# Key stacks completed by transfers inside SBUF, and sixteen attention rows scaled on another engine

## The chip, the cores and the metric

The kernel runs on one core of one Trainium2 chip. The metric is the device time of one execution in microseconds (us). Below, TensorE does matmuls (PE, its weight loads PEld), VectorE is DVE, ScalarE is ACT, GpSimd is POOL, and SyncE (SP) issues nearly all transfers (DMAs).

## What is computed

One transformer layer on 512 tokens of width 1024: a modulated layer norm, one projection to queries, keys, values and gates, two kinds of attention of 8 heads each, an output projection, a second norm and a gated feed-forward part with a short convolution. What matters here is the attention. Heads "a" use one softmax with a mask that merges three dilation patterns. Heads "b" have three branches (compressed, selected, window), each with a softmax of its own and a gate. In short:

```python
qa, ka, va, qb, kc, vc, ksl, vsl, kw, vw, gl = jnp.split(u @ w_in[l], split_at, axis=-1)
o_a = dilated_attention(partial_rope(heads(qa, N_HEADS_A), pos),
                        partial_rope(heads(ka, N_HEADS_A), pos), heads(va, N_HEADS_A))
...
s = jnp.einsum('bghqd,bgkd->bghqk', qc, kwc).astype(jnp.float32) * scale
p, _, den = masked_exp(s, wmask, -1)
o_win = jnp.einsum('bghqk,bgkd->bghqd', p, vwc) / den
o = gc[..., 0:1] * o_cmp + gc[..., 1:2] * o_slc + gc[..., 2:3] * o_win
```

## The kernel before, in words

**Products of halves.** To keep float32 accuracy a factor is split into a high part (a copy to fp32r) and a low part (the rest). The projections, which the trace calls "quad", multiply high by high, high by low and low by high (mm3, L259 to L261).

**Query and key stacks.** A head has 64 columns, so its transposed query fills 64 of 128 partitions. The kernel uses the other 64: q_stack writes the high part of a query in one half of the partitions and its low part in the other (L468 to L471). A key stack, made by k_half, holds the same key twice, once in each half of the partitions: khh has its high part twice, kll its low part twice. So one matmul with khh and one with kll, each contracting over all 128 partitions, give a row's scores (L700, L701). k_half takes the transposed key from PSUM: ScalarE writes the high part into both halves (L477, L478), VectorE subtracts to get the low part in one half (L479) and copies it into the other (L480). It is called twelve times: four times ahead of the first row (k_stack, keys of the selected and window branches for both groups), and twice for each of the head pairs a0 to a3 (in a_post, one step of the background work each).

**Rows.** A row is the work on one or two query tiles of 128 tokens of one head and branch: tiles (0, 1) with 128 + 256 = 384 score columns, tile 2 with 384, tile 3 with 512. The order of the heads is ROWS: b0, b1, a0, a1, b2, the compressed rows c, b3, a2, a3. Each of the heads b0 and b1 has 12 rows, so rows 0 to 23 are theirs, and all of them have a gate. A row goes through these steps: scores (TensorE), weights (VectorE: mask and row minimum, L708), power (ScalarE: exponential and its sum, L714), scale (VectorE: reciprocal of the sum, L719; GpSimd: times reciprocal times gate, in place, L722), turn (TensorE: transposes, L727), parts (ScalarE: high part, L746), rest (VectorE: low part, L750), use (TensorE: weighted sum of values, L775). Step k of the main loop has the scores of row k + 1, the mask and exponential of row k, the scaling of row k - 1, the transposes of row k - 3 and the weighted sum of row k - 5, and between these steps puts pieces of the projections (fill) and of the background work (misc).

**Projections and loads.** fill_stream loads a piece of w_quad into one of four raw buffers (wraw), splits it on ScalarE and VectorE (L1108, L1111) and multiplies. The same four buffers serve the modulation weights (ada_col, consumed by L1019 on VectorE; ada_row by L1010) and the compression weights (k_w, v_w). All of these loads are issued by SyncE, in order, and each waits until its buffer is free.

**Order.** The tile framework orders the instructions of each engine when the kernel is built, and sets the waits between engines. An engine then works its own list in that order.

Of the kernel before, what the change touches and what calls it, by code (L numbers as in the profile page):

```python
# [14 lines left out]
AF = mybir.ActivationFunctionType  # L15
# [91 lines left out]
def body(ctx, tc, nc, a, out, dbg=None):  # L107
# [59 lines left out]
    V, A, P, T = nc.vector, nc.scalar, nc.gpsimd, nc.tensor  # L167
# [23 lines left out]
    def q4(name, dt=F32, shape=(128, 1024)):  # L191
        return slot('q4', NQ, list(shape), dt, name)
# [16 lines left out]
    def pk(name):  # L209
        return slot('p', NP, [128, 512], F32, name)  # L210
# [22 lines left out]
    def bank(tag, name=None, shape=(128, 512)):  # L233
        return ps.tile(list(shape), F32, name=name or tag, tag=tag, bufs=BANKS[tag])

    def f(x):
        return x.bitcast(F32)

    def load(dst, src, queue=nc.sync):
        queue.dma_start(dst, src)  # L240
# [230 lines left out]
        V.tensor_sub(o[0:64], pt[64:128], f(o[64:128]))  # L471
        return e, o

    def k_half(pt, e, mk=t2):
        b, c0 = 64 * e, 64 - 64 * e
        hh, ll = mk('khh'), mk('kll')
        A.activation(hh[b:b + 64], pt[b:b + 64], AF.Copy)  # L477
        A.activation(hh[c0:c0 + 64], pt[b:b + 64], AF.Copy)  # L478
        V.tensor_sub(ll[b:b + 64], pt[b:b + 64], f(hh[b:b + 64]))  # L479
        V.tensor_copy(ll[c0:c0 + 64], f(ll[b:b + 64]))  # L480
        return hh, ll

    def k_stack(pt, mk=t2):
        return [k_half(pt, e, mk) for e in range(2)]


    gates = cst.tile([128, NT, 24], F32, name='gates')
# [194 lines left out]
    def attend(need_q, need_v, pv_of, qk_of, vsel, mask0, gate, first, last, end, f4):  # L682
# [3 lines left out]
        def row(tiles):  # L686
            cols, n = {}, 0
            for i in tiles:
                cols[i] = slice(n, n + 128 * (i + 1))
                n += 128 * (i + 1)  # L690
            pr, one = tiles[0] // 2, len(tiles) == 1
            e = {'n': n}

            def scores():
                need(*need_q)
                q, (hh, ll) = qk_of()
                e['s'] = bank('s', 'sp')
                for i in tiles:
                    qi = q[:, 128 * i:128 * i + 128]
                    T.matmul(e['s'][:, cols[i]], qi, hh[:, 0:128 * (i + 1)], start=True, stop=False)  # L700
                    T.matmul(e['s'][:, cols[i]], qi, ll[:, 0:128 * (i + 1)], start=False, stop=True)  # L701

            def weights():
                p = e['p'] = pk('p')
                m_ = e['m'] = cst.tile([128, 3, 2], F32, name='sa_', tag='sa_', bufs=5)
                for x, i in enumerate(tiles):
                    m0 = mask0 + 512 - 128 * (i + 1)
                    V.tensor_tensor_reduce(p[:, cols[i]], e['s'][:, cols[i]], masks[:, m0:mask0 + 512], 1.0, 3e38,  # L708
                                           op0=ALU.add, op1=ALU.min, accum_out=m_[:, 0, x:x + 1])

            def power():
                p, m_ = e['p'], e['m']
                for x, i in enumerate(tiles):
                    A.activation(p[:, cols[i]], p[:, cols[i]], AF.Exp, bias=m_[:, 0, x:x + 1], scale=-1.0,  # L714
                                 accum_out=m_[:, 1, x:x + 1])

            def scale():
                p, m_ = e['p'], e['m']
                V.reciprocal(m_[:, 2, 0:len(tiles)], m_[:, 1, 0:len(tiles)])  # L719
                for x, i in enumerate(tiles):  # L720
                    g = 1.0 if gate is None else gates[:, i, gate:gate + 1]
                    P.tensor_scalar(p[:, cols[i]], p[:, cols[i]], m_[:, 2, x:x + 1], g, op0=ALU.mult, op1=ALU.mult)  # L722

            def turn():
                e['t'] = bank('tr', 'pT')
                for j in range(n // 128):
                    T.transpose(e['t'][:, 128 * j:128 * j + 128], e['p'][:, 128 * j:128 * j + 128], ident)  # L727

            def side(c):
                if pr == 0:  # L730
                    return pair['h'][:, 512 * c:512 * c + 384]
                x = 128 * (tiles[0] % 2)
                return pair['hl'[c]][:, 0:n // 128, x:x + 128]

            def turned():
                t = e['t'][:, 0:n]
                return t if pr == 0 else t.rearrange("p (j q) -> p j q", q=128)

            def parts():
                if pr == 0:  # L740
                    pair['h'] = q4('pT', F32 if f4 else F32R)
                elif tiles[0] == 2:
                    pair['h'] = q4('pTh', F32 if f4 else F32R, (128, 4, 256))
                    if not f4:
                        pair['l'] = q4('pTl', F32R, (128, 4, 256))
                A.activation(side(0), turned(), AF.Copy)  # L746

            def rest():
                if not f4:
                    V.tensor_sub(side(1), turned(), f(side(0)))  # L750
                e['pair'] = dict(pair)
                if pr == 0:
                    lows.append(e['pair'])

            def use():
                if tiles[0] == LU:
                    return
                need(*need_v)
                if LU == 0 and tiles[0] == 2:
                    product_of(0, lows[0])  # L760
                else:
                    product_of(pr, e['pair'])

            def product_of(pr, tl):
                pv = pv_of()
                for j in range(2 * pr + 2):
                    o0 = 128 if j == 2 * pr + 1 else 0
                    o_ = pv[:, 256 * pr + o0:256 * pr + 256]
                    for c in range(1 if f4 else 2):
                        if pr == 0:  # L770
                            x = 512 * c + 256 * j
                            m_ = tl['h'][:, x:x + 256 - o0]
                        else:
                            m_ = tl['hl'[c]][:, j, o0:256]
                        T.matmul(o_, vsel(j), m_, start=(first and pr == 0 and j == 0 and c == 0),  # L775
                                 stop=(last and j == 3 and (f4 or c == 1)))
                if pr == 1:
                    end()

            e.update(scores=scores, weights=weights, power=power, scale=scale, turn=turn, parts=parts, rest=rest,  # L780
                     use=use)
            return e
# [257 lines left out]
    def late_steps(gap, AUX):  # L1040
        for c in AUX:
            if c == 'k':
                yield from hidden(kc_r, 'k_w1', P, comp_keys)
            if c == 'v':
                yield from hidden(vc_t, 'v_w1', P, comp_values)
            if c == 'g':
                yield from ada_row(0, g1l, gap)
            if c == 'c':
                yield from ada_late_cols(gap)
            if c == '2':  # L1050
                yield from ada_late_cols(gap, (2,))
            if c == '3':
                yield from ada_late_cols(gap, (3,))
# [10 lines left out]
    def start_misc(gen, early=False):  # L1064
        misc.insert(0 if early else len(misc), [0, gen])
# [116 lines left out]
    def need(*names):  # L1182
        while any(n not in ready for n in names):
            count(names)
            if fill_one() is fill:
                run_misc(True)
            elif tick[0] % 2:
                run_misc()
            else:
                tick[0] += 1  # L1190
# [53 lines left out]
    rows, done_b = [], []  # L1244
    for r in ROWS:
# [3 lines left out]
        else:  # L1249
            i = int(r[1])  # L1250
# [28 lines left out]
    for st_ in AUX:  # L1279
        start_misc(late_steps(GAP, st_))  # L1280
    nrow = len(rows)
    rows[0]['scores']()
    wo_started = [False]
    wo_fill = wo_first()
# [261 lines left out]
```

## Time and profile before

| | us |
|---|---|
| median of 3 runs | 726.68 |
| lowest, highest | 724.72, 728.5 |
| the profiled execution, own time | 726.39 |
| its span, first to last instruction | 724.6 |
| TensorE busy (matmuls) | 691.1 |
| VectorE busy | 464.8 |
| ScalarE busy | 345.7 |
| GpSimd busy | 248.7 |
| granted clock of TensorE, mean over the span | 0.99 |

The times of engines are sums over one profiled execution; they overlap. An engine's matmul ends are modelled, so a busy TensorE may still be slower than its peak. The granted clock is 1.00 at 2.4 GHz and 0.50 at 1.2 GHz. In the list of waits, a line names the waiting engine, its tile and line, then what ended the wait; then us in total, times, longest us. In a timeline, a line gives the start in us from the start of the span, the duration, engine, line, operation, tiles written and read, shapes, and in brackets the idle time of the engine just ahead of it with what ended it.

### The profile page before, as it was taken

How to read it: one execution, taken by the hardware profiler on the slowest of the kernel's cores; microseconds unless marked ns; L12 is line 12 of the kernel's file. 1: busy time of each engine (PE TensorE's matmuls, PEld its weight loads, DVE VectorE, ACT ScalarE, POOL GpSimd, SP SyncE). 2: the span in 40 equal slices, each digit the busy share in tenths (PEclk: the TensorE clock that was granted, in tenths of full speed). 3: DMA queues.
4: the chain of work that ended last, by engine and by line, in shares of the span. 5: the costliest groups of instructions: out<-in, count | busy, mean ns of one | idle time of the engine just before them, and what ended most of it. 6: DMA issues, size and time to landing. Idle time of an engine off the chain costs nothing.

```text
span 724.6 us, 10875 instructions
## 1 busy us (share of the span) xinstructions
PE 691.1 (95%) x3964; PEld 596.8 (82%) x3964; DVE 464.8 (64%) x961; ACT 345.7 (48%) x697; POOL 248.7 (34%) x273
## 2 busy tenths in 40 slices
PE   7999899999889998999999999999999999999995
PEld 6999788987879887778898888888888788888884
DVE  7879966766986889988843344464443364544236
ACT  5647665752767689916553333333333341222101
POOL 2002436441277475511310110111111355666216
PEclk9999999999999999999999999999999999999998
DMA  9955342046451011260112224434423233343002
GB/s 340 386 207 206 131 135 86 30 174 238 140 204 60 29 60 58 86 235 1 59 60 87 88 88 145 140 135 161 145 88 116 88 107 126 116 146 121 25 15 101
DMA packets 29149, 89.93 MB, mean 124 GB/s; under 512 B 3748, under 2 KB 4516, under 8 KB 29096
## 3 DMA queue, kind: packets, MB, share of 16 engines
q1 hardware_dynamic: 28660, 89.05, 35.6%
q8 instruction: 31, 0.51, 0.3%
q10 hardware_dynamic: 436, 0.18, 0.1%
q14 instruction: 22, 0.18, 0.1%
HBM read 87.13 MB, written 2.10 MB: 123 GB/s over the span
## 4 chain that ended last, share of the span: by engine, by line
PE 51%; DVE 3%; POOL 1%; issue 1%; ACT 0%; POOLq 0%; DVEq 0%
PE d L261 6%; PE d L260 6%; PE d L259 5%; PE pvv L259 5%; PE pvv L261 5%; PE pvv L260 5%; PE pg L259 5%; PE pg L261 5%; PE pg L260 5%; DVE x L1355 1%; PE wo L261 1%; PE wo L260 1%; PE wo L259 1%; DVE x L1346 0%; DVE bn L299 0%
## 5 line engine op out<-in xcount | busy, mean ns | idle before, releaser
L256 DVE TENSOR_TENSOR wlo<-wraw,whi 128x1024 fp32r<-128x1024 f32 x60 | 86.2, 1437 | 124.8 <-ACT whi L255 123.6
L255 ACT ACTIVATE whi<-wraw 128x1024 fp32r<-128x1024 f32 x60 | 63.6, 1060 | 142.9 <-PE pg L260 70.4
L259 PE MATMUL quad<-whi,u 128*128 128x256 f32 x256 | 75.0, 294 | 1.0 <-DVE qo L471 1.0
L260 PE MATMUL quad<-wlo,u 128*128 128x256 f32 x256 | 72.8, 284 | 0.0
L261 PE MATMUL quad<-whi,u 128*128 128x256 f32 x256 | 72.6, 284 | 0.0
L1498 POOL TENSOR_TENSOR wraw<-wraw,arow 128x1024 f32<-128x1024 f32 x22 | 57.8, 2633 | 35.3 <-DMA wraw<-w_down 28.6
L259 PE MATMUL pg<-u,whi 128*128 128x512 f32 (+1 forms) x176 | 67.7, 385 | 0.0
L260 PE MATMUL pg<-u,whi 128*128 128x512 f32 (+1 forms) x176 | 66.8, 380 | 0.0
L261 PE MATMUL pg<-u,wlo 128*128 128x512 f32 (+1 forms) x176 | 66.8, 379 | 0.0
L261 PE MATMUL pvv<-u,wlo 128*128 128x512 f32 (+1 forms) x176 | 66.8, 379 | 0.0
L259 PE MATMUL pvv<-u,whi 128*128 128x512 f32 (+1 forms) x176 | 66.8, 379 | 0.0
L260 PE MATMUL pvv<-u,whi 128*128 128x512 f32 (+1 forms) x176 | 66.8, 379 | 0.0
L256 POOL TENSOR_TENSOR hl<-cv,hh 128x512 fp32r<-128x512 f32 x14 | 23.9, 1705 | 110.8 <-ACT hh L255 110.8
L259 PEld LDWEIGHTS quad<-whi,u 128*128 128x128 f32 x256 | 48.7, 191 | 5.7 <-issue 3.9
L708 DVE CUSTOM_DVE_ANT_0 p<-sp,masks 128x128 f32<-128x128 f32 (+1 forms) x96 | 45.0, 482 | 8.8 <-PE sp L701 7.9
L260 PEld LDWEIGHTS quad<-wlo,u 128*128 128x128 f32 x256 | 48.9, 191 | 1.0 <-issue 0.4
L261 PEld LDWEIGHTS quad<-whi,u 128*128 128x128 f32 x256 | 48.9, 191 | 0.1
L727 PE MATMUL pT<-ident,p 128*128 128x128 f32 x240 | 39.8, 280 | 4.6 <-POOL p L722 4.2
L260 PEld LDWEIGHTS pg<-u,whi 128*128 128x128 f32 x176 | 33.1, 188 | 6.6 <-issue 0.5
L256 POOL TENSOR_TENSOR hg<-cv,hg 128x512 fp32r<-128x512 f32 x8 | 12.9, 1609 | 74.9 <-ACT hg L255 74.9
L259 PEld LDWEIGHTS pg<-u,whi 128*128 128x128 f32 x176 | 33.1, 188 | 6.6 <-issue 0.5
L261 PEld LDWEIGHTS pvv<-u,wlo 128*128 128x128 f32 x176 | 33.1, 188 | 6.3
(636 smaller groups left out, 1884.7 us busy)
## 6 DMA issues: line engine op xcount, KB each, us to landing
wraw<-w_up SPq DMA_DIRECT2D x44, 512.0 KB, 3.2
wraw<-w_down SPq DMA_DIRECT2D x22, 512.0 KB, 3.4
ada<-ada_col SPq DMA_DIRECT2D x32, 256.0 KB, 6.0
wraw<-w_quad SPq DMA_DIRECT2D x16, 512.0 KB, 4.9
wraw<-ada_col SPq DMA_DIRECT2D x16, 512.0 KB, 3.3
wraw<-ada_row SPq DMA_DIRECT2D x16, 512.0 KB, 3.6
x<-x SPq DMA_DIRECT2D x8, 512.0 KB, 4.8
wraw<-w_o SPq DMA_DIRECT2D x8, 512.0 KB, 3.2
```

The lines of the kernel that those rows point to most:

```text
L255: A.activation(hi, raw, AF.Copy)
L256: lo_engine.tensor_sub(lo, raw, f(hi))
L259: T.matmul(o_, sh, mh, start=start, stop=False)
L260: T.matmul(o_, sh, ml, start=False, stop=False)
L261: T.matmul(o_, sl, mh, start=False, stop=stop)
L708: V.tensor_tensor_reduce(p[:, cols[i]], e['s'][:, cols[i]], masks[:, m0:mask0 + 512], 1.0, 3e38, op0=ALU.add, op1=ALU.min, accum_out=m_[:, ...
L727: T.transpose(e['t'][:, 128 * j:128 * j + 128], e['p'][:, 128 * j:128 * j + 128], ident)
L1355: V.scalar_tensor_tensor(src[:, hs], src[:, hs], ag[:, 3:4], b_[h][:, cs], op0=ALU.mult, op1=ALU.add)
L1498: P.tensor_mul(w, w, g2)
```

## The change

k_half gets an argument `spare`, true for all calls. With it the second copies of khh and kll aren't written by ScalarE and VectorE: a transfer issued by SyncE copies the finished half of 64 partitions to the other half, 64 x 512 values of 4 bytes, 128 KB. Over twelve calls 12 ScalarE and 12 VectorE copies go, and 24 transfers come. In scale, rows 4 to 19 take another way: VectorE multiplies the reciprocal by the gate (one small instruction for each row, as all these rows have a gate), and ScalarE multiplies each tile by that value, in place. GpSimd's instruction for these rows goes.

```diff
--- before.py
+++ after.py
@@ -471,8 +471,15 @@
         V.tensor_sub(o[0:64], pt[64:128], f(o[64:128]))
         return e, o
 
-    def k_half(pt, e, mk=t2):
+    def k_half(pt, e, mk=t2, spare=True):
         b, c0 = 64 * e, 64 - 64 * e
+        if spare:
+            hh, ll = mk('khh'), mk('kll')
+            A.activation(hh[b:b + 64], pt[b:b + 64], AF.Copy)
+            load(f(hh[c0:c0 + 64]), f(hh[b:b + 64]))
+            V.tensor_sub(ll[b:b + 64], pt[b:b + 64], f(hh[b:b + 64]))
+            load(f(ll[c0:c0 + 64]), f(ll[b:b + 64]))
+            return hh, ll
         hh, ll = mk('khh'), mk('kll')
         A.activation(hh[b:b + 64], pt[b:b + 64], AF.Copy)
         A.activation(hh[c0:c0 + 64], pt[b:b + 64], AF.Copy)
@@ -717,6 +724,13 @@
             def scale():
                 p, m_ = e['p'], e['m']
                 V.reciprocal(m_[:, 2, 0:len(tiles)], m_[:, 1, 0:len(tiles)])
+                if e['act']:
+                    if gate is not None:
+                        g = gates[:, tiles[0]:tiles[-1] + 1, gate:gate + 1].rearrange("p t o -> p (t o)")
+                        V.tensor_mul(m_[:, 2, 0:len(tiles)], m_[:, 2, 0:len(tiles)], g)
+                    for x, i in enumerate(tiles):
+                        A.activation(p[:, cols[i]], p[:, cols[i]], AF.Copy, scale=m_[:, 2, x:x + 1])
+                    return
                 for x, i in enumerate(tiles):
                     g = 1.0 if gate is None else gates[:, i, gate:gate + 1]
                     P.tensor_scalar(p[:, cols[i]], p[:, cols[i]], m_[:, 2, x:x + 1], g, op0=ALU.mult, op1=ALU.mult)
@@ -1279,6 +1293,8 @@
     for st_ in AUX:
         start_misc(late_steps(GAP, st_))
     nrow = len(rows)
+    for k, r in enumerate(rows):
+        r['act'] = 4 <= k < 20
     rows[0]['scores']()
     wo_started = [False]
     wo_fill = wo_first()
```

## Rows read from the trace of the kernel before

**Rows 1.** The page's busy list: busy us, share of the span, instructions.
```profile
PE 691.1 (95%) x3964; PEld 596.8 (82%) x3964; DVE 464.8 (64%) x961; ACT 345.7 (48%) x697; POOL 248.7 (34%) x273
```

**Rows 2.** Stretches: length, busy (count) of PE, PEld, DVE, ACT, POOL, clock, DMA.
```profile
75.00:78.43 3.43, 1.47 (x5) 0.77 (x5) 3.31 (x10) 1.82 (x7) 0.38 (x1) 1.00 0.19 75
78.43:81.85 3.42, 3.26 (x15) 3.27 (x15) 3.42 (x16) 1.81 (x7) 2.58 (x3) 0.50 0.00 0
88.00:133.00 45.00, 43.21 (x324) 38.73 (x323) 32.03 (x96) 26.41 (x75) 22.02 (x35) 1.00 0.32 105
247.00:256.00 9.00, 6.20 (x47) 5.51 (x46) 8.72 (x27) 5.99 (x17) 0.72 (x2) 1.00 0.01 2
...
310.00:720.00 410.00, 404.10 (x1882) 336.67 (x1880) 209.11 (x274) 140.46 (x218) 120.66 (x82) 1.00 0.30 103
```

**Rows 3.** TensorE's waits over the span: total us, times, longest us.
```profile
PE pT L727 <- POOL p L722: 4.2, 4, 2.6
...
PE pcT L665 <- POOL pc L660: 1.5, 1, 1.5
```

**Rows 4.** TensorE's waits from 88 to 133 us, the whole list.
```profile
PE pvb L775 <- DVE y L803: 1.8, 1, 1.8
```

**Rows 5.** TensorE's timeline: the first scores of rows 0 and 1.
```profile
71.34 0.30 PE L700 MATMUL sp<-khh,qe 128*128 128x128 f32 x1 [1.11 <-DVE qo L471]
...
76.17 0.45 PE L700 MATMUL sp<-khh,qe 128*128 128x384 f32 x1 [1.27 <-DVE sa__982 L708]
```

**Rows 6.** VectorE's timeline at the start of attention: low parts of the keys.
```profile
64.72 0.68 DVE L479 TENSOR_TENSOR kll<-qT,khh 64x512 fp32r<-64x512 f32 x1
65.32 0.67 DVE L1111 TENSOR_TENSOR wlo<-wraw,whi 128x512 fp32r<-128x512 f32 x1
66.02 0.42 DVE L480 CAST kll<-kll 64x512 fp32r<-64x512 f32 x1
...
68.90 0.90 DVE L480 CAST kll<-kll 64x512 fp32r<-64x512 f32 x1
...
73.14 0.86 DVE L480 CAST kll<-kll 64x512 fp32r<-64x512 f32 x1
...
75.09 0.58 DVE L480 CAST kll<-kll 64x512 fp32r<-64x512 f32 x1
```

**Rows 7.** DMA issues, over the span and 62 to 72: KB each, us to landing.
```profile
o<-x SPq DMA_DIRECT2D x1, 160.0 KB, 2.1
...
wraw<-ada_col SPq DMA_DIRECT2D x3, 512.0 KB, 4.7
```

**Rows 8.** The instructions of L478: duration ns min/median/max, first and last start.
```profile
L478 ACT ACTIVATE khh<-qT x12: 588/592/597, 62.9 to 281.5; 64x512 fp32r<-64x512 f32 x12
```

**Rows 9.** Timelines of VectorE, TensorE and SyncE around the keys of a0, a1.
```profile
142.01 0.68 DVE L479 TENSOR_TENSOR kll<-qT,khh 64x512 fp32r<-64x512 f32 x1 [1.23 <-PE pvb L775]
...
186.79 0.68 DVE L479 TENSOR_TENSOR kll<-qT,khh 64x512 fp32r<-64x512 f32 x1
...
144.07 0.22 PE L700 MATMUL sp<-khh,qe 128*128 128x128 f32 x1
...
189.88 0.22 PE L701 MATMUL sp<-kll,qe 128*128 128x128 f32 x1
...
185.42 4.38 SPq L240 DMA_DIRECT2D wraw<-ada_col  x3
```

**Rows 10.** ScalarE's timeline: exponentials of 384 and 512 columns.
```profile
93.36 0.61 ACT L714 ACTIVATE p<-p,sa__1233 128x384 f32<-128x384 f32 x1
...
93.95 0.71 ACT L714 ACTIVATE p<-p,sa__1271 128x512 f32<-128x512 f32 x1
```

**Rows 11.** The reciprocals of L719 alone, by stretch: length, VectorE busy (count), clock, DMA.
```profile
88.00:133.00 45.00, 2.48 (x16) 1.00 0.32 105
```

**Rows 12.** ScalarE's waits from 88 to 133 us for the masking, longest and shortest.
```profile
ACT p L714 <- DVE sa__1583 L708: 1.2, 1, 1.2
...
ACT p L714 <- DVE sa__1357 L708: 0.6, 1, 0.6
```

## The prediction

> **What bounds the kernel now.** I start from the page's busy list: TensorE is busy 691.1 us of a span of 724.6 [rows 1], so only some 33 us can be won without removing matmuls, and the change removes none. The table by stretches then says where they lie. From 310 us to 720 us TensorE works 404.1 us of 410 [rows 2]; the change touches nothing there. So all of it must happen in the attention stage, from about 60 to 310 us. There I read the list of TensorE's waits, longest total first. Transposes that wait for GpSimd's scaling (L722) are at its head with 4.2 us in four waits [rows 3], which looks like the thing that the second edit attacks. But the scaled rows 4 to 19 are worked at about 88 to 133 us, and the same list cut to that stretch has one entry, 1.8 us, for a VectorE add (L803) and not for the scaling [rows 4]: there the scaling is hidden already. The other place is the start of attention. The timeline of TensorE shows row 0's scores waiting 1.11 us for VectorE's last query split (L471) and row 1's scores 1.27 us for VectorE's masking of row 0 (L708) [rows 5]. VectorE is busy 3.31 of 3.43 us at 75 to 78.43 us while TensorE has 1.47 [rows 2]: this short stretch is VectorE's. Right behind it the granted clock falls to 0.50, the 1.2 GHz level, for 3.42 us [rows 2].
>
> **Edit 1, key stacks, start of attention.** Twelve calls of k_half lose one ScalarE copy (L478) and one VectorE copy (L480) each and gain two transfers of 64 partitions x 2 KB, 128 KB, on SyncE's queue. Four calls lie at the start. Their VectorE copies took 0.42, 0.90, 0.86 and 0.58 us [rows 6], 2.76 us in all, in the chain that sets rows 0 to 2: the first two (1.32 us) stand before L471, the other two (1.44 us) before the masking of row 0. Taking out 1.32 us ends row 0's wait of 1.11, and the next 1.44 ends row 1's 1.27 [rows 5], so the upper bound is 2.76 us if VectorE's lane simply closes up. The lower bound is 4 x 0.42 = 1.7 us, the copy's undisturbed price: the excess over 0.42 may pass on to whatever VectorE does next. (The Trainium skill, SBUF — State Buffer, section "Who interferes with whom", says that a VectorE copy and a GpSimd instruction lock each other out of a shared port pair for the whole instruction; 0.90 beside 0.42 agrees. By that rule the excess goes only where the next VectorE instruction doesn't want the pair, and the sum would use 1.7.) I take 2.3, the middle.
>
> What replaces the copies must not come later than VectorE. The score matmul contracts over all 128 partitions, so it needs both landed halves. The first low half can leave when L479 ends, 64.72 + 0.68 = 65.4 us [rows 6]. No transfer inside SBUF stands in the trace; the nearest by size is an output store of 160 KB, 2.1 us from issue to landing, and the nearest by place are the loads of 62 to 72 us, 4.7 us [rows 7]. That gives 67.5 to 70.1 us, and row 0 would want it at about 71.34 - 1.3 = 70.0: just in time, cost 0. The removed ScalarE copies (0.59 us each [rows 8]) matter little here: ScalarE isn't what the scores wait for.
>
> **Edit 1, heads a0 and a1.** Here the keys are used at once. For a0 the low half was split at 142.01 for 0.68 us, and the first score started at 144.07 [rows 9]. The split stood right behind L478, so with that copy of 0.59 us [rows 8] gone it could start at 141.4; it ends at 142.1, and its transfer lands 2.1 to 4.7 us later, at 144.2 to 146.8. Against 144.07 that is 0.1 to 2.7 us late. I take a value near the small end, +0.5, since the store's row is the nearest in size; it is unhidden, since TensorE's work behind that score follows in order. (The Trainium skill, DMA: Bandwidth & Descriptors, section "Anatomy of one DMA — SWDGE (gpsimd) path", gives about 2.0 us fixed plus bytes over 436 GB/s, an estimate of 2.3 us here, for a path issued by GpSimd and not by SyncE; by it the landing is at 144.4 and this term +0.3; no run so far shows such a transfer.) For a1 the split ends at 187.47, so landing is at 189.6 to 192.2, against the low half's first matmul at 189.88 [rows 9]: 0 to 2.3 us, and I take +0.7, as loads run beside it. Other cover: projection matmuls ("quad") stand between the scores, and an order that puts more of them ahead makes both terms 0.
>
> **Edit 1, heads a2 and a3.** Their keys are made under other heads' rows, well ahead of their own first scores, so a landing some us later is hidden. VectorE is nearly full there, 8.72 of 9 us at 247 to 256, while TensorE has 6.20 [rows 2] and waits 1.5 us for the compressed row (L660) whose inputs VectorE makes [rows 3]. Four copies of 0.42 leave: 0 to 1.7 us. I take half, -0.8.
>
> **Edit 1, the queue.** SyncE issues in order, so each transfer that stands for L477 or L479 holds the weight loads queued behind it (w_quad, ada_col, k_w), and is held by loads that stand for a free buffer. Those who would wait for a late load are the splits L1108 and L1111. Three ada_col loads at 185.42 took 4.38 us to be issued, waiting for VectorE [rows 9]; a key transfer behind the last of them would leave at about 189.8 and not 187.5. I cost it at nothing in the forecast, since loads run ahead of their splits, and at up to 2.3 more for a1.
>
> **Edit 2, rows 4 to 19.** Sixteen rows leave GpSimd: five with two tiles, six of 384 and five of 512 columns, 21 instructions. ScalarE's exponential of the same shapes took 0.61 us at 384 and 0.71 at 512 columns [rows 10]; going down by 0.10 per 128 I estimate 0.40 and 0.51 for the two tiles. That is 5 x 0.91 + 6 x 0.61 + 5 x 0.71 = 11.8 us more for ScalarE, which has 26.4 of 45 us at 88 to 133 [rows 2]: 38.2 of 45, still not full. VectorE gets 16 small products; 16 reciprocals on as few columns took 2.48 us there [rows 11], so I add 2.5 us to 32.0 of 45 [rows 2]. Ahead of the change TensorE loses 1.8 us there at all [rows 4], so the gain is 0 to 1.8. The added wait stands on ScalarE: its scaling waits for VectorE's reciprocal and product, with the exponentials and the copies of the transposes (L746) queued behind, for which TensorE's weighted sums wait. I take 0.
>
> **Sum.** -2.3 + 0.5 + 0.7 - 0.8 + 0 = -1.9 us. The profiled run took 726.39 us (span 724.6, 1.8 around it), 0.3 under the median of 726.68, less than the runs differ by; so **724.5 us**. This measurement tells about 0.5% from no change, 3.6 us: faster is under 723.0, slower over 730.3.
>
> **Rivals.**
> *The clock stays up, and more waits close.* With its 2.4 us of waits gone, TensorE may be busy enough before 78.43 us that the clock doesn't fall. In that stretch its matmuls were busy 3.26 us at half clock [rows 2]; at the full one they would take about half, so some 1.6 us come back. With the full 2.76 and 1.7, and a0 and a1 covered by projections, 726.4 - 2.76 - 1.6 - 1.7 = 720.3. For it: right before the fall TensorE had been busy 1.47 of 3.43 us [rows 2], which the edit makes denser. Against: all three gains must come in full. Chance 0.34.
> *ScalarE sets the pace of rows 4 to 19.* 45 - 38.2 = 6.8 us of room is 0.43 us a row. ScalarE already stands for VectorE in that stretch, in eight waits from 1.2 down to 0.6 us, 0.86 on the mean [rows 12]. If each row's scaling costs one such wait, 16 x (0.86 - 0.43) = 6.9 us, giving 726.4 - 1.9 + 6.9 = 731.4. It decides from 0.43 us a row. Against it: scores run four rows ahead of the transposes, and the order can put another row's work first. Chance 0.16.
> *Transfers come late.* a0 at its 2.7, a1 at 2.3 + 2.3, the rest as forecast: 726.4 - 2.3 - 0.8 + 7.3 = 730.6 at the worst, and half of that delay gives 727. Chance 0.10, a third of it slower.
> *Nothing of it reaches the path*, because the order of instructions on an engine isn't that of the source: between L479 and its copy L480 another piece (L1111) ran [rows 6]. If the waits only move, 726.4 stays. Chance 0.08.
> The forecast keeps 0.32, nearly all of it within 0.5%.
>
> **Chances and range.** Faster 0.35 (the clock case and the edge of the forecast), same 0.45 (forecast, no effect, two thirds of late transfers, and parts of the others), slower 0.20 (ScalarE's pace and late transfers). The range is 719.5 to 731.5: from a little under the first rival, since edit 2 can give up to 1.8, to the second rival.
>
> **What would show it.** Right: rows 0 and 1 of the scores start 1 us or more sooner with their waits for L471 and L708 gone; key transfers land 2 to 3 us after issue; TensorE's waits at 88 to 133 us stay under 2 us with ScalarE near 38 of 45. Wrong: scores that wait for a key transfer; a clock that falls elsewhere; long waits of ScalarE for the reciprocal with TensorE waiting for L746 or L750 behind; or a different order of engines' work that moves waits into the projections.

## The result, and the profile after

The change makes the kernel a little faster. Over seven runs of each the median went from 726.58 to 721.82 us, a ratio of 0.9932 (95% interval 0.9916 to 0.9948), or some 4.9 us. A second set of runs of the same two kernels gave 0.9934 (0.9917 to 0.9952). The forecast was 724.5 us. The time lies near the first rival's 720.3 us, though, as the experiments show, not for all of its reasons. It is under the 723.0 that the prediction called faster, a case to which it gave 0.35, against 0.45 for no clear change.

The profiled run of the changed kernel is the slowest of its seven, 724.09 us with a span of 722.3; where a reading depends on that, the profile of the second set (720.97 us, span 719.2) is used, called "the whole change again". In the changed kernel scores are L707 and L708 (before: L700, L701), the mask L715 (L708), reciprocal, gate product, ScalarE's and GpSimd's scaling L726, L730, L732, L736 (L719, L722), a key's low part L480 (L479), the modulation sum L1033 (L1019). The page's busy list answers [rows 1]:

```profile
PE 692.0 (96%) x3964; PEld 598.6 (83%) x3964; DVE 459.2 (64%) x965; ACT 347.3 (48%) x706; POOL 238.7 (33%) x252
```

TensorE's work is unchanged, as it must be; VectorE lost 5.6 us, ScalarE gained 1.6 and GpSimd lost 10. The table by stretches answers [rows 2], with the same columns:

```profile
75.00:78.43 3.43, 3.43 (x30) 3.43 (x30) 0.76 (x1) 0.88 (x3) 0.95 (x2) 1.00 0.63 206
78.43:81.85 3.42, 2.13 (x17) 1.89 (x16) 3.42 (x13) 1.64 (x6) 0.26 (x1) 1.00 0.50 157
88.00:133.00 45.00, 43.92 (x330) 39.43 (x330) 33.21 (x115) 36.37 (x98) 9.62 (x15) 1.00 0.29 99
```

TensorE now has 30 matmuls at 75 to 78.43 us instead of 5, and the granted clock stays at 1.00 behind it. The timeline of TensorE answers [rows 5], row 0 and row 1:

```profile
69.53 0.22 PE L707 MATMUL sp<-khh,qe 128*128 128x128 f32 x1
71.84 0.44 PE L707 MATMUL sp<-khh,qe 128*128 128x384 f32 x1 [0.37 <-DVE qo L471]
```

Row 0 starts 1.8 us sooner and row 1 4.3 us sooner; 0.5 us of each was there at 59 us already. Row 1 no longer waits for the mask of row 0. VectorE's timeline shows why, and answers [rows 6] (the mask at 71.82 us is row 0's first):

```profile
62.84 0.67 DVE L480 TENSOR_TENSOR kll<-qT,khh 64x512 fp32r<-64x512 f32 x1
63.58 1.27 DVE L1033 CUSTOM_DVE_ANT_0 wraw<-wraw,crow,b_col 128x1024 f32<-128x1024 f32 x1
64.88 0.69 DVE L480 TENSOR_TENSOR kll<-qT,khh 64x512 fp32r<-64x512 f32 x1
...
68.36 1.27 DVE L1033 CUSTOM_DVE_ANT_0 wraw<-wraw,crow,b_col 128x1024 f32<-128x1024 f32 x1
69.67 0.69 DVE L480 TENSOR_TENSOR kll<-qT,khh 64x512 fp32r<-64x512 f32 x1
...
71.09 0.69 DVE L471 TENSOR_TENSOR qo<-qT,qo 64x512 fp32r<-64x512 f32 x1
71.82 0.29 DVE L715 CUSTOM_DVE_ANT_0 p<-sp,masks 128x128 f32<-128x128 f32 x1
...
77.67 1.29 DVE L1033 CUSTOM_DVE_ANT_0 wraw<-wraw,crow,b_col 128x1024 f32<-128x1024 f32 x1 [2.87 <-DMA wraw<-ada_col]
```

Three things are new. The four copies are gone, and so is one more piece. In the kernel before, three modulation sums stand around the key splits and ahead of the first mask, and the second query split (its end is L471) stands behind that mask, in its timeline:

```profile
63.38 1.28 DVE L1019 CUSTOM_DVE_ANT_0 wraw<-wraw,crow,b_col 128x1024 f32<-128x1024 f32 x1
...
66.84 1.28 DVE L1019 CUSTOM_DVE_ANT_0 wraw<-wraw,crow,b_col 128x1024 f32<-128x1024 f32 x1 [0.40 <-DMA wraw<-ada_col]
...
71.83 1.27 DVE L1019 CUSTOM_DVE_ANT_0 wraw<-wraw,crow,b_col 128x1024 f32<-128x1024 f32 x1
...
74.76 0.29 DVE L708 CUSTOM_DVE_ANT_0 p<-sp,masks 128x128 f32<-128x128 f32 x1
...
76.84 0.69 DVE L471 TENSOR_TENSOR qo<-qT,qo 64x512 fp32r<-64x512 f32 x1
```

Now there are two sums, and the third stands behind three rows' masks. There VectorE is idle for 2.87 us, since the load of that sum, issued at 70.90 us behind eight key transfers, landed at 77.53. The masks of row 3 stand behind it, and row 5's scores wait 1.3 us for them. The list of TensorE's waits over the span, with the columns of [rows 3], names both new kinds of wait:

```profile
PE sp L708 <- DMA kll<-kll: 1.3, 2, 0.9
PE sp L707 <- DVE sa__1095 L715: 1.3, 1, 1.3
```

The third new thing is the place of the second query split. Before, row 1 waited for row 0's mask, and row 2 for this split behind it, in TensorE's timeline:

```profile
77.59 0.50 PE L700 MATMUL sp<-khh,qe 128*128 128x512 f32 x1 [0.68 <-DVE qo L471]
```

Now the split stands ahead of row 0's mask; row 1 waits 0.37 us for it, and row 2 doesn't wait for it. It goes together with the clock: of the fourteen profiles of this case, the eight without a stretch at half clock between 70 and 100 us all have the split ahead of row 0's mask, and the six with one all have it behind. No run moves this split alone, so what hangs on it is not shown.

### The profile page after: what moved, and what is told of

The parts are those of the page before. It is cut to its first block, busy times and chain, and to the rows that moved or that the text cites. A ratio compares the mean times of both kernels' runs of the same rounds, so it can differ in the third digit from the quotient of the medians.

```text
span 722.3 us, 10901 instructions
## 1 busy us (share of the span) xinstructions
PE 692.0 (96%) x3964; PEld 598.6 (83%) x3964; DVE 459.2 (64%) x965; ACT 347.3 (48%) x706; POOL 238.7 (33%) x252
## 4 chain that ended last, share of the span: by engine, by line
PE 75%; DVE 11%; ACT 5%; POOL 3%; issue 3%; DMA 2%; POOLq 0%; SPq 0%; DVEq 0%; ACTq 0%
PE d L261 6%; PE d L260 6%; PE d L259 6%; PE pvv L259 5%; PE pvv L261 5%; PE pvv L260 5%; PE pg L259 5%; PE pg L261 5%; PE pg L260 5%; PE first L393 3%; PE quad L259 3%; PE quad L260 2%; PE quad L261 2%; PE pT L741 2%; PE hid L1160 2%
## 5 line engine op out<-in xcount | busy, mean ns | idle before, releaser
L256 DVE TENSOR_TENSOR wlo<-wraw,whi 128x1024 fp32r<-128x1024 f32 x60 | 83.7, 1395 | 122.6 <-ACT whi L255 121.4
L715 DVE CUSTOM_DVE_ANT_0 p<-sp,masks 128x128 f32<-128x128 f32 (+1 forms) x96 | 44.6, 482 | 8.6 <-PE sp L708 8.2
L261 PEld LDWEIGHTS pg<-u,wlo 128*128 128x128 f32 x176 | 33.1, 188 | 6.3
L260 PEld LDWEIGHTS pvv<-u,whi 128*128 128x128 f32 x176 | 33.1, 188 | 6.2
```

The costliest lines, as they stand in the source:

```text
L256: lo_engine.tensor_sub(lo, raw, f(hi))
L260: T.matmul(o_, sh, ml, start=False, stop=False)
L261: T.matmul(o_, sl, mh, start=False, stop=stop)
```

## The experiments

Each kernel is compared with the kernel before on the same chip. The table puts the runs beside two places of their profiles: the first score of row 1, and a projection matmul at 100.4 us of the kernel before, both as a shift against it (us, corrected for the shift at 59 us, worked out from TensorE's timelines), and whether the profile has a stretch at granted clock 0.50 between 70 and 100 us.

| kernel | ratio (95% interval) | row 1 | at 100 us | half clock |
|---|---|---|---|---|
| both_again | 0.9934 (0.9917 to 0.9952) | -3.8 | -3.3 | none |
| keys_alone | 0.9936 (0.9914 to 0.9957) | -3.1 | -4.1 | none |
| keys_start | 0.9937 (0.9918 to 0.9955) | -3.8 | -2.7 | none |
| rows_alone | 0.9974 (0.9956 to 0.9991) | -0.2 | -0.4 | 77.27 to 80.69 |
| ll_start | 1.0015 (0.9992 to 1.0038) | -0.5 | +2.0 | 77.78 to 84.60 |
| hh_start | 0.9981 (0.9959 to 1.0004) | -2.0 | +0.4 | 80.09 to 83.51 |
| lane_back | 0.9987 (0.9969 to 1.0005) | -2.0 | -1.1 | 75.42 to 78.83 |
| ll_start_all | 0.9994 (0.9977 to 1.0010) | -0.2 | +2.0 | 76.49 to 83.31 |
| cols_late | 0.9959 (0.9941 to 0.9977) | -2.2 | -3.5 | none |
| both_cols_late | 0.9959 (0.9944 to 0.9973) | -5.2 | -4.4 | none |
| keys_cols_late | 0.9932 (0.9912 to 0.9952) | -5.1 | -4.5 | none |
| keys_twice | 0.9996 (0.9974 to 1.0017) | -2.6 | -2.8 | none |

**Which edit.** The whole change once more, each edit alone, and the key edit at the start only.

```diff
 rows_alone:  def k_half(pt, e, mk=t2, spare=False):
 keys_alone:  r['act'] = False
 keys_start:  r['act'] = False, spare=False, and in k_stack
-        return [k_half(pt, e, mk) for e in range(2)]
+        return [k_half(pt, e, mk, True) for e in range(2)]
```

> The whole change once more, as the measure for its parts on the same chip. Before took 726.58 us, the change 721.82, so -4.8 us. If that is the change's own, this run is again 4 to 5.5 us under before; if part of it was luck of the runs, it is nearer to the -1.9 us that the prediction summed.

> All twelve key stacks by transfers, the scaling of all rows left on GpSimd. My theory (the terms of the prediction's sum): -2.3 at the start, +1.2 at a0 and a1, -0.8 at a2 and a3, so -1.9 us against before. Rival that the rows carry the gain: at most -1 us. Rival that the clock at the start is what counts: -3.5 us or more, with the stretch at 1.2 GHz near 78 us gone in its profile.

> Rows 4 to 19 scaled by ScalarE, the key stacks as before. My theory: 0 us, at best -1.8. The rival from the trace after the change, in which TensorE's wait for the add at the end of head b1 (1.8 us before) is missing: about -2 us, with that wait gone here too. If the parts add, keys alone and rows alone together give the -4.8 us of both; if a new order of instructions is the cause, they don't add, by 1.5 us or more.

> Only the four key stacks ahead of row 0 by transfers; those of a0 to a3 and all rows as before. My theory: -2.3 us against before (VectorE's 1.7 to 2.8 us leave the chain that sets rows 0 to 2), and so about 0.4 us more gain than all keys, since a0 and a1 cost and a2 and a3 give. The rival that only the later keys count: 0 us.

The medians were 722.18, 721.65, 725.04 and 722.50 against 726.37 us. So the four calls of k_stack carry what the key edit gives; the eight later calls add nothing that these ratios show. The rows alone give 0.26% and add nothing beside the keys. keys_alone came out as its clock rival had it, and rows_alone near its rival, with the wait for the add gone. By the ratios the two parts alone make 6.5 us and the whole 4.8; the 1.7 us between them lie within the noise of three ratios, so whether the parts add is not decided.

**Which of the two copies.** At the start only one half of a key stack by transfer: the low part (VectorE loses its copies, ScalarE keeps its own), or the high part (the reverse). Then both by transfer, but VectorE gets its four copies back, writing to a tile that nobody reads.

```diff
 ll_start, ll_start_all:
-            load(f(hh[c0:c0 + 64]), f(hh[b:b + 64]))
+            A.activation(hh[c0:c0 + 64], pt[b:b + 64], AF.Copy)
 hh_start:
-            load(f(ll[c0:c0 + 64]), f(ll[b:b + 64]))
+            V.tensor_copy(ll[c0:c0 + 64], f(ll[b:b + 64]))
 lane_back:
+            V.tensor_copy(to('spent')[c0:c0 + 64], f(ll[b:b + 64]))
```

> Only the four key stacks at the start of attention are changed, and of each only the low part: its second half comes by a transfer, the second high part is still ScalarE's copy. Rows 4 to 19 stay on GpSimd. Theory (VectorE's lane sets rows 0 to 2, and what follows at half clock goes with it): VectorE loses the same four copies as in keys_start, so the time is 3 to 4 us under the kernel before, row 1's first scores start some 4 us earlier than 76.17 us, and the stretch at half clock from 78.43 us is gone. Since four transfers instead of eight stand in SyncE's queue, the loads behind them come earlier, so it may be up to 1 us better than keys_start. Rival (both copies matter, ScalarE's too): half the gain, about -2 us.

> The other half of the edit alone: at the start of attention the second high part comes by a transfer and the second low part is VectorE's copy as before. Theory (VectorE's lane): row 1's scores still wait for VectorE's masking of row 0, the half clock from about 78 us stays, and the time is the kernel before's within 1 us; the transfers gain nothing because the scores don't wait for ScalarE. Rival (ScalarE's copies or a new order of the instructions did it): 2 us or more under the kernel before.

> The four key stacks at the start by transfers, as in keys_start, and VectorE is given a copy of the same size and place as the one removed, into a tile that nothing reads. So transfers, order of loads and ScalarE are those of keys_start and only VectorE's lane has its old price. Theory (lane): the gain of keys_start (-3.9 us) is gone, 0 within 1 us, and the half clock from about 78 us is back. Rival (the gain comes from what the transfers free in the order, scores no longer held behind the masking of row 0): it keeps 2 us or more.

> The whole change, except that at the start of attention the second high parts stay with ScalarE (four transfers fewer there). Theory: the key transfers at the start delay the modulation weights behind them, for which VectorE stood 1.0 to 2.9 us in the profiles of the whole change; with half of them gone the time is 0.5 to 1.3 us under the whole change, 720.5 to 721.5. Rival (that delay is hidden, or ScalarE's four copies take it back): the same as the whole change, 721.8 to 722.2, or over it.

The theory (VectorE's lane, emptied of its copies) failed on ll_start: with VectorE's four copies gone the time was 726.82 against 725.80 us, no gain at all, where 3 to 4 us were expected. Its timeline of VectorE says why:

```profile
63.27 1.28 DVE L1033 CUSTOM_DVE_ANT_0 wraw<-wraw,crow,b_col 128x1024 f32<-128x1024 f32 x1
64.61 0.68 DVE L480 TENSOR_TENSOR kll<-qT,khh 64x512 fp32r<-64x512 f32 x1
66.34 1.28 DVE L1033 CUSTOM_DVE_ANT_0 wraw<-wraw,crow,b_col 128x1024 f32<-128x1024 f32 x1 [0.45 <-DMA wraw<-ada_col]
...
72.44 1.63 DVE L1033 CUSTOM_DVE_ANT_0 wraw<-wraw,crow,b_col 128x1024 f32<-128x1024 f32 x1 [1.94 <-DMA wraw<-ada_col]
74.00 0.28 DVE L715 CUSTOM_DVE_ANT_0 p<-sp,masks 128x128 f32<-128x128 f32 x1
```

The sums have kept the places that they have in the kernel before, ahead of the first key split and of the first mask. The time that the copies gave free went into waiting for the load of the third, 1.94 us. Its buffer was free at 67.63 us, but it was issued at 68.90: SyncE stood ahead of it for a key transfer that waited for the low part split at 67.66 us. The high part's transfer alone (hh_start) moves one sum out, and row 1 is 2.0 us sooner, but the work at 100 us is 0.4 us behind, and the gain of 0.19% has an interval that reaches no change. The half clock stayed, as expected for it; the time, 1.4 us less by the ratio, lies between its theory and its rival. Only both together have the short lane. lane_back then prices VectorE's copies: with the transfers of keys_start and the sums in the same places, but the copies back, row 1 starts 1.8 us later (-2.0 instead of -3.8), the stretch at half clock returns and most of the gain goes. The second query split stands behind row 0's mask again there, so the price is that of the copies together with this change of order. ll_start_all, meant as an improvement, falls for the same reason as ll_start: it is no better than the kernel before, where 720.5 to 721.5 us were expected.

**Order alone.** The new theory is that half of the gain is not the copies but the modulation sums that leave VectorE's lane. So no transfer at all: the sums of the kernel before start later. Then the same with the whole change, and with the keys only.

```diff
-    for st_ in EAUX:
-        start_misc(late_steps(GAP, st_))
...
+        if k == 4:
+            for st_ in EAUX:
+                start_misc(late_steps(GAP, st_))
```

> The kernel before, key copies and rows untouched; only the start of one piece of background work is put off: the eight sums of modulation columns (ada_col, 1.28 us each on VectorE) begin in step 4 of the main loop and not ahead of row 0. Theory (the edit gains because VectorE's lane ahead of rows 0 to 2 gets shorter, half of it by an order in which fewer of these sums stand between the key splits): three of the sums, 3.8 us, leave the lane without any transfer of keys, row 1's scores start 2 to 4 us earlier than 76.17 us, the half clock from 78 us goes, and the time is 2 to 4 us under the kernel before. Rival (the key copies themselves are what costs, or the sums cost the same wherever they stand): within 1 us of the kernel before.

> The whole change and the same putting off of the modulation sums. Theory: the loads of these sums, behind which VectorE stood 1.0 to 2.9 us in the profiles of the whole change, are out of the stretch too, so it is 1 to 2.5 us under the whole change (722), near 720. Rival (that wait is covered, or the sums now crowd rows 4 to 19, where VectorE was busy 32 of 45 us): 722 or more.

> As the run before, but rows 4 to 19 stay on GpSimd: a second look at what the scaling on ScalarE is worth beside the key edit, where the first pair showed nothing (722.2 with it, 721.7 without). If it is worth the 1.3 us that it gave alone, this run is 1 to 2 us over the one before; if the gain of 2 us near 127 us is given back behind it, the two agree within 1 us.

cols_late took 723.21 against 726.63 us, 0.41% less, with all copies in place and no transfer. Row 1 is 2.2 us sooner, and the clock doesn't fall where it fell before, as its table by stretches shows:

```profile
75.00:78.43 3.43, 3.43 (x29) 3.25 (x28) 3.42 (x17) 2.98 (x11) 3.02 (x5) 1.00 0.00 0
78.43:81.85 3.42, 3.42 (x24) 2.65 (x23) 2.92 (x9) 2.39 (x6) 1.69 (x4) 1.00 0.47 152
```

So order alone is worth some 60% of the change. Order means here the sums with their loads, and the second query split, which stands ahead of row 0's mask in this kernel too. The profile is that of the slowest of its twelve runs (727.54 us): there the clock falls at 113.62 us instead, and a matmul at 120 us of the kernel before is 1.6 us late, so the profile shows the start alone, and the 0.41% rests on the twelve times. Two of the three sums left the lane and not all, since the framework drew one ahead again. Beside the whole change it gave nothing: 723.87 us with the rows on ScalarE, where about 720 were expected, and 721.82 without. The second is 2.0 us under the first, which neither of the two cases written down for it had. Row 1 was another 1.3 us sooner there, but that did not reach the end: with the late sums in rows 4 to 19, TensorE waits for the add (L817) there again, 2.3 us with the rows on ScalarE, in the list from 88 to 133 us:

```profile
PE pvb L789 <- DVE y L817: 2.3, 2, 1.7
```

**The price of the transfers.** keys_start with each key transfer issued twice.

```diff
             load(f(hh[c0:c0 + 64]), f(hh[b:b + 64]))
+            load(f(hh[c0:c0 + 64]), f(hh[b:b + 64]))
...
             load(f(ll[c0:c0 + 64]), f(ll[b:b + 64]))
+            load(f(ll[c0:c0 + 64]), f(ll[b:b + 64]))
```

> keys_start with each of the eight key transfers at the start issued twice, the second a repeat of the first: 16 transfers, 1 MB more on SyncE's queue there, nothing more on any other engine. Theory (the transfers and the loads held behind them are late by some us but mostly covered by projection matmuls): the scores wait longer for a low half than the 0.4 us in keys_start, and the modulation loads come later; 0.5 to 2 us over keys_start (722.5), still under the kernel before. Rival (transfers cost nothing, as costed in the prediction): the same as keys_start within 1 us. Rival (they are what limits the start now, 4.6 to 6.9 us each): 3 us or more over it, the gain gone.

It took 725.38 against 726.23 us: the gain is gone, some 3 us by the medians, 4 by the ratios, near the second rival. The list of TensorE's waits from 60 to 100 us of keys_twice has two entries, both new:

```profile
PE hid L1162 <- DMA wraw<-k_w: 1.6, 1, 1.6
PE sp L709 <- DMA khh<-khh: 1.1, 1, 1.1
```

1.6 us is a compression weight (k_w) whose load was held in SyncE's queue, and 1.1 us a score that waited for its key. But these 2.7 us stand in place of 2.0 us of other waits in keys_start: at 100 us the work is 2.8 us ahead of the kernel before, as in keys_start (2.7), at 192 us 2.0 against 1.8, and the two profiled runs took 725.24 and 726.34 us. So the profiles don't show where the gain went. The mean granted clock of the runs was 0.9861, against 0.9910 in keys_start; by the rate that is estimated below this would be 2.3 us, but why it was lower no run shows. That doubling the transfers costs time is shown; how, and what one transfer costs, is not.

## Why the prediction was right or wrong

**Where the bound lies** was right: TensorE's busy time stayed, and keys_start, which changes the start of attention alone, has the whole gain within the runs' noise.

**Key stacks at the start, -2.3 (bounds 1.7 to 2.76).** The term was mis-sized, and its reason was incomplete. The copies, with the second query split behind the mask, are worth 1.8 us at row 1 (lane_back), at the low end of the bounds. What the prediction treated as a fixed background, the order of VectorE's other work, changed with the edit and gave another 2.0 us at row 1. It also took the query split that row 0 waits for as the last one; the second stands behind row 0's mask, and row 2 waited 0.68 us for it. The prediction had named the order as a thing that could take the gain away ("nothing of it reaches the path") and not as one that could add to it.

**The clock.** The forecast left the stretch at half clock where it was. It went, as the first rival said. In the eight profiles without it (the changed kernel and those marked "none") the work at 100 us is 2.7 to 4.5 us ahead, but for the changed kernel's own, 0.7 us, where VectorE stood for the late load; in the five others with it, between 1.1 ahead and 2.0 behind. How much of this is the clock itself is an estimate. Over 85 runs of the kernel before, the median was 728.59 us in the 11 with a mean granted clock of 0.983 and 725.29 in the 26 with 0.990, 0.47 us for each 0.001. The changed kernel's seven runs had 0.9896 on the mean against 0.9876 in those 85, so some 0.9 us. The rival had 1.6. The estimate is loose: keys_alone has the same ratio at 0.9883, which would be 0.3 us, and keys_start at 0.9910, 1.6. The rival is thus right that the clock stays up at 78 us, and that a0 and a1 are covered, but the order carries much of what the rest of its sum gave to the copies. Other half-clock stretches fall at different places: at 184 us before, at 186 and 203 us after, and at 114 to 126 us in keys_alone, keys_start, keys_twice and cols_late. Before and after, the profiles thus have two such stretches of 3.4 us each between 60 and 310 us, and no single profile gives the whole difference.

**Transfers landing in time, cost 0.** They took longer than the prediction had it at the start, and stayed inside its bounds later, mostly at the lower end. The changed kernel's answer for SyncE's transfers of the low halves gives the least, the median and the longest of the five, out of twelve, whose landing shows:

```profile
DMA to landing us min/median/max: 2.2/3.3/5.8
```

At the start the four, of both halves, whose landing shows took 5.2 to 6.9 us, beyond the 4.7 of the loads in [rows 7]. Row 0 shows no wait for that, since projection matmuls stand ahead of it; row 3 waits 0.9 us.

**Heads a0 and a1, +0.5 and +0.7.** a0's scores waited 0.2 and 0.5 us for its halves in the profiled run, 0.2 in keys_alone and not at all in the whole change again; a1's never. +0.5 was about right at its worst, +0.7 was not there: the projections covered it, as the last sentence of that part allowed.

**Heads a2 and a3, -0.8.** The wait of [rows 3] for the compressed row did close, as TensorE's waits from 240 to 310 us of the changed kernel show:

```profile
PE pT L741 <- DVE pTl L764: 1.8, 2, 1.4
...
PE pcT L672 <- POOL pc L667: 0.2, 1, 0.2
```

From 1.5 us to 0.2; but transposes near it now wait 1.8 us for VectorE's low parts (L764), a wait that the kernel before doesn't have in this stretch. By the list alone a stall was exchanged for another. The places of TensorE's work say more: from a projection matmul at 219.6 us of the kernel before to the first feed-forward matmul (pg) at 351.5, each of the six profiles with all later keys by transfer gains 0.7 to 0.9 us on it, both of the whole change 0.9, and the seven others are within 0.1 but for rows_alone, which loses 1.6 and has a stretch at half clock at 278.66 us. So -0.8 was about right. That keys_alone and keys_start have the same ratio doesn't speak against it, since their intervals are wider than that.

**The queue, 0.** Wrong. The loads behind the key transfers came late, VectorE stood 2.87 us (1.0 in the whole change again, where the same load landed 4.8 us after its issue and not 6.6), and row 5's scores 1.3 us. The prediction watched the splits L1108 and L1111 as those who would wait, and missed the modulation sums, which take loads from the same queue.

**Rows 4 to 19, 0 (-1.8 to 0).** Right, with a mechanism that the bounds held. ScalarE was busy 36.4 of 45 us against the 38.2 worked out; its 384-column scaling took 0.61 and the 512-column one 0.71 to 0.73 us, as estimated from the exponentials. The wait of [rows 4] for the add is gone in the whole change again, whose list from 88 to 133 us has one entry:

```profile
PE pT L741 <- ACT p L732: 0.4, 1, 0.4
```

Alone, the edit gives 1.9 us (0.65 to 3.2). But beside the keys it gave nothing twice: 722.18 with it and 721.65 without, and 723.87 against 721.82 in the kernels with late sums. A part of the gain is given back just behind, in the whole change again from 134 to 140 us: transposes (L462) that waited 0.3 us for VectorE's query split in the kernel before wait 1.3 us now.

```profile
PE qT L462 <- DVE qo L471: 1.3, 1, 1.3
```

So 1.0 of the 1.8 us is given back within some 12 us. rows_alone has the same wait, 1.2 us, so it isn't what sets the two cases apart. Why the edit shows alone and not beside the keys stays open. The rival "ScalarE sets the pace" did not happen: its waits for the gate product (L730) were 1.3, 0.7 and less, and TensorE waited for ScalarE's scaling 1.1 us in one profile and 0.4 in the other.

**The sum.** -1.9 was forecast and -4.9 measured. The time came out inside the range, but with a gain over twice the forecast's, by an order that the forecast didn't have. By the places of TensorE's work, corrected for 59 us as in the table, the whole change again is 3.3 us ahead at 100 us, 5.3 at 134, 4.6 at 164, 4.0 at 219 (with one stretch at half clock more than the kernel before since 164), and 4.9 from 351 us to the end. So the start gives most of it, the rows give 2.0 and lose 0.7 of it behind, and heads a2 and a3 give 0.9. What in the 3.3 us is copies, order or clock isn't separated: the 1.8 and 2.0 us at row 1 aren't shares of the end, since hh_start has the 2.0 whole and is 0.4 us behind at 100 us.

## What to carry to other kernels

When a framework orders the instructions, an edit changes two things, the work and the order; ask which other work stands in the lane of the chain, and try moving that work alone first, since here it gave some 60% of the gain with no transfer of keys. A transfer that replaces a copy can be paid by whoever waits for the loads queued behind it, so list every consumer of that queue and not only those nearest the edit. When a stall is taken away, look right behind it for the wait that takes its place, and compare the place of later work before calling the two even: a list of waits hid 0.9 us here.

## What the runs showed of the hardware

A gate product of one or two columns on VectorE (L730) took 0.14 to 0.16 us in 13 of the 16 rows of the changed kernel, but 0.68 and 0.69 us in two and 0.32 in one; the two in VectorE's timeline:

```profile
89.06 0.68 DVE L730 TENSOR_TENSOR sa__1128<-sa__1128,gates 128x1 f32<-128x1 f32 x1
...
90.22 0.15 DVE L726 RECIPROCAL sa__1164<-sa__1164 128x1 f32<-128x1 f32 x1
...
90.97 0.69 DVE L730 TENSOR_TENSOR sa__1164<-sa__1164,gates 128x1 f32<-128x1 f32 x1
```

At both places GpSimd was working through additions of 0.7 to 1.6 us each (L519) with hardly a pause, from 85.62 to 93.67 us, and in the whole change again three long products (0.68 to 0.70 us) lie inside the same work; the reciprocal between them kept its 0.15 us. In these two profiles and those of rows_alone, both_cols_late and ll_start_all, each of the 15 products that took over 0.25 us ends 0.02 us behind the end of a GpSimd instruction beside it. ScalarE's longest wait for a gate product, 1.3 us, ends behind the first of the two shown. No run took the two engines apart, so the cause is read from these coincidences alone. The Trainium skill, SBUF — State Buffer, section "Who interferes with whom", has the rule for it: a VectorE instruction with two inputs in SBUF takes its second one through a read port shared with GpSimd and can wait for a GpSimd instruction that reads SBUF, while one with at most one such input does not, outside the modes that use both port pairs. The product has two such inputs, the reciprocal one; the trace agrees.

Transfers of 128 KB inside SBUF, issued by SyncE, took 2.2 to 2.3 us from issue to landing at 246 to 282 us, and 5.2 to 6.9 us at 63 to 76 us, where 512 KB loads stand in the same queue (4.1 to 5.4 there in keys_alone).
